# Sums of squares by 32x32 turning on VectorE, state-space values turned by VectorE and DRAM, a third of the weights' low parts on GpSimd

## The chip, the cores and the metric

One core of one Trainium2 chip runs the kernel. The metric is the device time of one execution in microseconds (us). Before the change it is 924.06 us, the median of three runs (923.71 to 925.14).

## The reference, cut to what matters

Two layers on x of 512 tokens by 1024 features. Each layer normalizes x and memory, makes one combined projection, feeds four groups of heads (retention, a Mamba-2 state-space part, stick-breaking attention, a read of 256 memory tokens), gates each group's 512 outputs, concatenates them, projects back and adds the normalized result to x.

```python
def hybrid_layer(x, mem, ...):
    hn = rmsnorm(x, pre_g)
    (ret_q, ret_k, ret_v, ret_g, xbc, z, dt_raw, sb_q, ...) = split(hn @ w_in)
    y_ret = retention(ret_q, ret_k, ret_v) * silu(ret_g)
    y_ssd = ssd_mixer(xbc, z, dt_raw, ...)
    ...
    y = concatenate([y_ret, y_ssd, y_sb, y_mem]) @ w_out
    return x + rmsnorm(y, post_g)
```

Three pieces bear on the change. Retention ends in a normalization of each of its 4 heads over 128 features. The state-space part ends in a root-mean-square norm over each of its 2 groups of 256 features. And it multiplies its convolved inputs by a step width per token and head:

```python
    # retention
    y = (y - mu) * rsqrt(var + EPS)             # mu, var over a head's 128 features
    # ssd_mixer
    xs, bm, cm = split(silu(conv(xbc) + conv_b))
    xdt = xs * delta                            # per token and head
    y_diag = (cc @ bm.T * decay_in) @ xdt       # within a chunk of 128 tokens
    states = bm.T @ (xdt * decay_states)        # one per chunk, then a running sum
    y = y_diag + (cc @ prev) * exp(a_cs) + xs * d_skip
    y = rmsnorm(y * silu(z))                    # per group of 256 features
```

## The kernel before, in words

Everything is float32, and a product of two float32 matrices is made of three matmuls: each operand is split into a high part (`h`) and a low part (`l`) of the type fp32r, and `mm3` adds `h*h`, `h*l` and `l*h`. Matmuls of this kind stand under L285 in the profile. A projection (`proj_b`) multiplies one sub-block of the weights, 1024 by 128, with all 512 tokens: 24 matmuls of 512 columns into one PSUM bank `pj`. Activations lie with features on partitions and tokens along the columns.

**Weights.** The weights of both layers are 156 sub-blocks, 78 per layer (`2 * NBLK`), of 1024 columns but for 12. ScalarE's DMA queue loads two sub-blocks at a time (`w_load`, tile `raw`). `w_prefetch` splits up to five sub-blocks ahead (`NSUB`): ScalarE casts the raw weight to `wh` (L293) and VectorE subtracts to get `wl` (L294), in 5 buffers each. After each projection one buffer of each is free for the next sub-block.

**The order of the work.** The code runs through the projections. `defer(n, f)` puts a step `f` off until `n` units later; `tick` counts one unit for each `proj_b` (two for `proj_a`) and runs what is due. A tile scheduler orders each engine's instructions when the kernel is built, by what they need and when they were written, so the order on an engine follows the units only roughly. Each engine then works in that order, one instruction behind the other, and the DMAs that SyncE (SP) issues go into its queue in its order too.

**The state-space part** (`ssd_group`, once for each of two groups, one behind the other). Its units are projections: two x blocks, a gate, B, C, a gate, two z blocks. `conv` makes a convolution of four taps with three VectorE products (L940) and a last one with a tanh (L943). The convolved values must have tokens on partitions for the products with chunk states: `ssd_values` transposes them on TensorE, 8 transposes per group of 128 by 128 by a matmul with the identity (L1003, 32 in all), into PSUM tiles `mx`, and VectorE multiplies those by the step widths (L1007) and by the decays (L1009). B is turned in another way, by `columns_turned`: VectorE's transpose of 32 by 32 blocks (`STREAM_TRANSPOSE`, L660), four DMAs on SyncE's queue that write its pieces to DRAM at their turned places (L663), and one DMA that reads the tile back (L668). `ssd_mix` multiplies the decay tiles with C by B (L1020), `ssd_states` makes three chunk states with a running product and sum on VectorE (the sum is L1033), and `ssd_out` makes the outputs (L1048 to L1056; it loads its own decays from DRAM in tiles `E`, L1041). `ssd_mix` of group 1 follows the tail of group 0 on VectorE.

**The norms.** `ssd_var` of a group, 5 units after the group's last z projection, squares both outputs on ScalarE and adds them on VectorE down to 64 partitions (L1063, L1064); it splits these into a high and a low part (L1067) and sums over the partitions with one matmul by a column of ones (`onesr`), which gives one row of 512 sums. `row_rstd` brings the row to 32 partitions of 16 values by a copy and a DMA (L811), adds epsilon and takes the power -0.5 on GpSimd (L812, L813), writes the row to DRAM (L815) and reads it back, broadcast to 128 partitions (L818, tile `r`). `ssd_norm`, 9 units after the z projection, scales the outputs by it on VectorE (L1075). Retention does the same for two heads at a time: `ret_head2` squares and adds to 32 partitions and splits, `ret_head3` makes the sums 3 units later, and `scaled` multiplies 7 units after that (L886).

GpSimd makes low parts at two places already, of activations: in `mem_head2` (L675, 16 subtractions of 128 by 512) and in `sb_head2` (L759, 24 of 256 to 512 columns).

Of the kernel before, what the change touches and what calls it, by code (L numbers as in the profile page):

```python
# [16 lines left out]
P = 128  # L17
# [117 lines left out]
def shape_constants():  # L135
    c = np.zeros((P, NCON), np.float32)
    i = np.arange(P)
    c[:, 0:128] = np.eye(P)
    c[:, 128:256] = i[:, None] <= i[None, :]
    c[:, 256:384] = 1.0  # L140
    c[:, 384:896] = np.arange(512)[None, :] < 383 + i[:, None]
    inv = np.float32(10000.0) ** (-np.arange(0, HD, 2, dtype=np.float32) / np.float32(HD))
    ang = (np.arange(SEQ, dtype=np.float32)[:, None] * inv[None, :].astype(np.float32)).T
    c[:, 896:1408] = np.concatenate([np.cos(ang), np.cos(ang)])
    c[:, 1408:1920] = np.concatenate([np.sin(ang), -np.sin(ang)])
    gam = 1.0 - 2.0 ** (-5.0 - np.arange(HEADS, dtype=np.float64))
# [4 lines left out]
    er = er.T.reshape(2, 2 * RP, RJ)  # L151
    c[:2 * RP, 1936:1968] = er.transpose(1, 0, 2).reshape(2 * RP, 2 * RJ)
    return c

BLK = 32
TT = "y"
ST, SL, SB1, SB2 = "s", "y", 2, 4
ROW = 128  # L160

# [13 lines left out]
class Builder:  # L175
# [4 lines left out]
    def __init__(self, tc, pools, args, taps=None):  # L180
        self.tc, self.nc = tc, tc.nc
        self.a = args
        self.taps = taps or {}
        self.fix, self.slots, self.small, self.wp, self.ps, self.dr = pools
        self.n = self.unit = 0
        self.todo, self.tanhs = [], []
        self.C = self.fixed(NCON + DEPTH * NPAR, F32, "consts")
        self.mhalf = self.fixed(RJ, F32, "mhalf")
        self.eps4 = self.fixed(RJ, F32, "eps4")
        self.b16 = self.fixed(2 * P, BF16, "b16")  # L190
        self.onesr = self.fixed(P, F32R, "onesr")
        self.nc.gpsimd.memset(self.mhalf[:], -0.5)
        self.nc.gpsimd.memset(self.eps4[:], EPS)

# [117 lines left out]
    def w_prefetch(self, upto=None, between=()):  # L312
        if self.starting and upto is None:
            return
        while self.w_split < (upto or min(self.nsubs, self.w_cur + self.NSUB)):
            k = self.w_split
            self.w_load(k // 2)
            n = block_width(k // 2) // 2
            h, l = (self.wp.tile([P, SUBW], F32R, tag=t, name=self.name(t), bufs=self.NSUB)[:, :n] for t in ("wh", "wl"))
            r = self.raw[k // 2]  # L320
            if isinstance(r, list):
                pieces = [(r[2 * (k % 2) + i][:], slice(512 * i, 512 * i + 512)) for i in range(2)]
            else:
# [12 lines left out]

    def w_load(self, b):
        while self.w_dma <= min(b, DEPTH * NBLK - 1):
# [461 lines left out]
        p.f = A  # L800
        return p

    def row_rstd(self, rows, eps, n=1):


        nc = self.nc
        e = self.buf(tag="r")[0:n]
        nc.scalar.copy(e, rows)
        c = self.tiny(RJ)[:n * RP]
        for i in range(n):  # L810
            nc.sync.dma_start(c[RP * i:RP * i + RP], e[i:i + 1].rearrange("o (p j) -> o p j", j=RJ))  # L811
        nc.gpsimd.tensor_tensor(out=c, in0=c, in1=eps, op=ALU.add)  # L812
        nc.gpsimd.tensor_tensor(out=c, in0=c, in1=self.mhalf[:n * RP], op=ALU.pow)  # L813
        d = self.dr.tile([n, SEQ], F32, tag=f"row{n}", name=self.name("row"), bufs=2)[:]
        nc.sync.dma_start(d.rearrange("o (p j) -> (o p) j", j=RJ), c)  # L815
        out = [self.buf(tag="r") for _ in range(n)]
        for i in range(n):
            nc.sync.dma_start(out[i], d[i:i + 1].to_broadcast([P, SEQ]))  # L818
# [32 lines left out]
    def ret_head2(self, h, v, sc, f, st, q, y):  # L851
# [10 lines left out]
        nc.scalar.copy(y, b)  # L862
        sq = self.buf(tag="r")
        nc.scalar.activation(sq, b, AF.Square, scale=HD ** -0.5)
        for n in (64, 32):
            nc.vector.tensor_add(sq[0:n], sq[0:n], sq[n:2 * n])
        if h % 2 == 0:
            self.z = self.new(512, F32R, "r"), []
# [8 lines left out]
    def ret_head3(self, i, z, ys):  # L877

        vb = self.mx()[0:2]
        self.mm(vb, self.onesr[:, 2:4], z[:], True, True)  # L880
        self.defer(7, self.scaled, ys, self.row_rstd(vb, self.con("reps", 2 * RJ, 2 * RP)[:, RJ * i:RJ * i + RJ], 2))

    def scaled(self, ys, rB):

# [74 lines left out]
    def ssd_group(self, l, g, ysb):  # L959
# [34 lines left out]
    def ssd_values(self, X):  # L994
# [1 line left out]
        nc, g = self.nc, X["g"]  # L996
        X["xdt"], X["xds"] = [], []
        for i in range(2):
            b = self.mx()
            for c in (2 * i, 2 * i + 1):  # L1000
                for j in range(2):
                    o = 256 * (c % 2) + P * j
                    nc.tensor.transpose(b[:, o:o + P], X["x"][j][:, P * c:P * c + P], self.con("ident", P))  # L1003
# [54 lines left out]
    def ssd_var(self, X):  # L1058
# [141 lines left out]
    def start(self):  # L1200
# [70 lines left out]
        self.first = self.proj_a(SSD_H, late)  # L1271
        self.mem_k2(k[1])
        self.w_load(6)
        nc.vector.tensor_copy(self.onesr[:], self.con("ones", P))

        nc.vector.tensor_copy(self.onesr[:, 2:3], self.con("tri", P)[:, 63:64])
        nc.vector.tensor_sub(self.onesr[:, 3:4], self.con("ones", 1), self.con("tri", P)[:, 63:64])

    def layer(self, l):
        self.exp_ln_phase()  # L1280
# [54 lines left out]
```

## Time and profile before

| what | value |
|---|---|
| median of three runs | 924.06 us |
| the profiled execution: its time | 923.25 us |
| its span, from the first to the last instruction | 921.5 us |
| granted TensorE clock, of full speed | 0.998 |
| low parts of weights on VectorE, 1024 wide (L294) | 144 of 1257 ns |
| all low parts of weights on VectorE | 156, 188.6 us |
| DMA rate, mean over the span | 139 GB/s |

A row of the profile's groups gives line, engine, operation, the tiles (out<-in, buffer numbers left out), partitions by elements and type, and a count; then the busy time in us and the mean of one in ns; then the idle time of that engine just before these instructions, and what ended most of it. A row of the timeline gives the start in us from the start of the span, the duration (of each, or of the whole run of like records), the engine, the line, the operation and a count; in square brackets the wait ahead of it and what ended it. A row of the chain has the same form, with the time that the chain spent there. PE is TensorE's matmul, PEld its weight load, DVE VectorE, ACT ScalarE, POOL GpSimd, SP SyncE; SPq is the DMA issue on SyncE's queue. The durations of matmul records overlap, so starts are compared and not durations.

### The profile page before, as it was taken

To read this page: it belongs to the slowest core of one execution; us is meant where nothing else is said; L and a number is where in the kernel's file an instruction comes from. 1 tells how busy PE (TensorE), PEld (TensorE's weight loads), DVE (VectorE), ACT (ScalarE), POOL (GpSimd) and SP (SyncE) were. 2 spreads that over 40 slices of the span, in tenths; PEclk is the share of its full clock that TensorE was granted. 3 is DMA by queue.
4 is the path that set the end of the run, shared out by engine and by line. 5 is a ranking of instruction groups with operands and counts; after the bars stand their busy time and mean duration, and the time that the engine had idled before them with its cause. 6 is when DMAs were issued, how large, how long until landed. Compare 5 with 4: busy or idle time off the path is not lost.

```text
span 921.5 us, 12952 instructions
## 1 busy us (share of the span) xinstructions
PE 913.2 (99%) x4667; PEld 773.6 (84%) x4667; DVE 673.3 (73%) x1081; ACT 443.5 (48%) x841; POOL 146.3 (16%) x208
## 2 busy tenths in 40 slices
PE   9999999999999999999999999999999999999997
PEld 7998888888888888888899888888888888888885
DVE  6855689888787887844587476898778869687343
ACT  6643485744453342733465336675445434335341
POOL 1200152320131110100040002423112120102001
PEclk9999999999999999999999999999999999999999
DMA  8544664642444333444345256556333362422502
GB/s 316 213 141 144 169 167 104 199 146 61 120 134 148 116 109 126 137 149 158 116 173 196 93 172 183 124 122 183 103 109 116 110 194 92 139 95 88 210 12 91
DMA packets 105408, 128.53 MB, mean 139 GB/s; under 512 B 64640, under 2 KB 79744, under 8 KB 96256
## 3 DMA queue, kind: packets, MB, share of 16 engines
q10 hardware_dynamic: 10224, 73.44, 23.4%
q1 hardware_dynamic: 95120, 54.28, 20.7%
q8 instruction: 36, 0.59, 0.3%
q14 instruction: 28, 0.23, 0.1%
HBM read 112.10 MB, written 15.56 MB: 139 GB/s over the span
## 4 chain that ended last, share of the span: by engine, by line
PE 98%; DMA 1%; ACT 0%; DVEq 0%; SPq 0%; POOLq 0%; issue 0%; POOL 0%; ACTq 0%; DVE 0%
PE pj L285 74%; PE mx L285 23%; PE mx L479 1%; DMA mem<-memT 1%; PE mx L1003 0%; ACT s L523 0%; DVEq L1331 0%; ACT s L1168 0%; POOLq L1331 0%; ACT wh L293 0%; SPq L506 0%; SPq L349 0%; SPq L1206 0%; POOL t L449 0%; ACTq L1331 0%
## 5 line engine op out<-in xcount | busy, mean ns | idle before, releaser
L285 PE MATMUL pj<-hTh,wh 128*128 128x512 f32 x704 | 276.4, 393 | 0.0
L285 PE MATMUL pj<-hTh,wl 128*128 128x512 f32 x704 | 275.8, 392 | 0.0
L285 PE MATMUL pj<-hTl,wh 128*128 128x512 f32 x704 | 274.6, 390 | 0.0
L294 DVE TENSOR_TENSOR wl<-raw,wh 128x1024 fp32r<-128x1024 f32 (+2 forms) x156 | 188.6, 1214 | 116.9 <-ACT wh L293 115.7
L293 ACT CAST wh<-raw 128x1024 fp32r<-128x1024 f32 (+2 forms) x156 | 158.7, 1020 | 205.0 <-PE pj L285 177.5
L285 PEld LDWEIGHTS pj<-hTh,wl 128*128 128x128 f32 x704 | 132.2, 188 | 27.3
L285 PEld LDWEIGHTS pj<-hTh,wh 128*128 128x128 f32 x704 | 132.3, 188 | 27.1 <-DVE s L593 0.8
L285 PEld LDWEIGHTS pj<-hTl,wh 128*128 128x128 f32 x704 | 132.3, 188 | 26.6
L285 PE MATMUL pj<-wh,s 128*128 128x512 f32 x320 | 97.6, 391 | 0.0
L285 PE MATMUL mx<-s,s 128*128 128x256 f32 (+4 forms) x528 | 79.7, 307 | 0.0
L285 PE MATMUL mx<-wh,s 128*128 128x512 f32 x256 | 79.2, 389 | 0.0
L285 PEld LDWEIGHTS mx<-s,s 128*128 128x128 f32 (+1 forms) x528 | 65.8, 177 | 8.2 <-PE pj L285 1.4
L285 PEld LDWEIGHTS pj<-wh,s 128*128 128x128 f32 x320 | 59.7, 188 | 12.4
L285 PE MATMUL pj<-wl,s 128*128 128x512 f32 x160 | 60.2, 389 | 0.0
L285 PEld LDWEIGHTS mx<-wh,s 128*128 128x128 f32 x256 | 48.1, 188 | 10.0
L294 DVE TENSOR_TENSOR s<-y,s 128x512 fp32r<-128x512 f32 x64 | 41.2, 687 | 19.7 <-ACT s L293 14.0
L262 ACT ACTIVATE s<-s 128x128 f32<-128x128 f32 (+3 forms) x96 | 41.8, 478 | 22.3 <-DVE s L733 20.6
L675 POOL TENSOR_TENSOR s<-y,s 128x512 fp32r<-128x512 f32 x16 | 23.7, 1494 | 179.9 <-ACT s L674 179.4
L293 ACT CAST s<-y 128x512 fp32r<-128x512 f32 x64 | 36.6, 617 | 30.8 <-PE mx L285 22.0
L285 PE MATMUL mx<-wl,s 128*128 128x512 f32 x128 | 49.6, 389 | 0.0
L285 PE MATMUL pj<-wl,hTh 128*128 128x256 f32 (+2 forms) x144 | 47.6, 331 | 0.0
L285 PE MATMUL pj<-wh,hTl 128*128 128x256 f32 (+2 forms) x144 | 47.5, 330 | 0.0
(185 smaller groups left out, 1298.5 us busy)
## 6 DMA issues: line engine op xcount, KB each, us to landing
raw<-wts ACTq DMA_DIRECT2D x69, 1024.0 KB, 4.8
s<-x SPq DMA_DIRECT2D x24, 256.0 KB, 4.1
y<-turned SPq DMA_DIRECT2D x24, 256.0 KB, 2.8
turned<-y SPq DMA_DIRECT2D x64, 64.0 KB, 2.2
s<-acs SPq DMA_DIRECT2D x16, 256.0 KB, 6.3
r<-row SPq DMA_DIRECT2D x12, 256.0 KB, 5.0
raw<-wts SPq DMA_DIRECT2D x4, 512.0 KB, 7.5
raw<-wts SPq DMA_DIRECT2D x2, 1024.0 KB, 6.3
```

The lines of the kernel that those rows point to most:

```text
L262: i = self.nc.scalar.activation(out, in_, func, **k)
L285: return self.nc.tensor.matmul(out, lhsT, rhs, start=start, stop=stop)
L293: self.nc.scalar.copy(h, src)
L294: self.nc.vector.tensor_sub(l, src, hf)
L479: x = self.nc.tensor.transpose(b[:, P * j:P * j + P], hn[i][:, P * j:P * j + P], self.con("ident", P))
L675: nc.gpsimd.tensor_sub(p.l, x, p.hf)
```

## The change

Four things change.

1. *State-space values.* `ssd_group` now calls `columns_turned` for the two convolved x tiles: two VectorE transposes, eight DMA writes and two DMA reads for each group, into two new tiles. `ssd_values` works on these in place in SBUF, three units after (`VD`) where it was two. The 32 transposes on TensorE are gone.
2. *Sums of squares.* The tree of additions goes down to 32 partitions. `row_rstd` takes these 32 rows (64 for a pair of retention heads), turns them in blocks of 32 by 32 on VectorE and adds along the columns with one reduction; so partition p holds the sums of the tokens p, p + 32, p + 64 and so on, 16 of them. Addition, power, write and broadcast follow as before, but the write puts each value at its own place in the row, 4 bytes apart by 128 bytes: 512 pieces, one DMA for each head. The copy, the DMA L811, the splits and the eight sums by matmul (4 of one row, 4 of two rows) are gone, with `ret_head3` and `onesr`. The table of retention's epsilons (`er`) is laid out anew to match.
3. *Units.* Retention scales 6 units (`RD`) after the second head's squares, where it was 3 + 7. `ssd_var` moves from 5 to 6 units and `ssd_norm` from 9 to 10.
4. *Low parts of weights.* `low_by_pool` names every third sub-block from the 14th on, but not those from the 16th to the 33rd of each layer's 78: 36 of the 156. For these GpSimd subtracts instead of VectorE.

TensorE has 4436 matmuls in its program where it had 4476 (40 fewer), and SyncE issues 473 DMAs where it issued 441.

```diff
+VD = 3
+RD, RT = 6, "r"
-TT = "y"
+TT, TX = "y", "s"
...
-                self.split(x, h[:, c], l[:, c], h[:, c].bitcast(F32))
+                nc = self.nc
+                nc.scalar.copy(h[:, c], x)
+                (nc.gpsimd if self.low_by_pool(k) else nc.vector).tensor_sub(l[:, c], x, h[:, c].bitcast(F32))
...
+    def low_by_pool(self, k):
+        return k > 12 and k % 3 == 2 and not 16 <= k % (2 * NBLK) < 34
...
-    def row_rstd(self, rows, eps, n=1):
+    def row_rstd(self, z, eps, n=1):
-        e = self.buf(tag="r")[0:n]
-        nc.scalar.copy(e, rows)
-        c = self.tiny(RJ)[:n * RP]
-        for i in range(n):
-            nc.sync.dma_start(c[RP * i:RP * i + RP], e[i:i + 1].rearrange("o (p j) -> o p j", j=RJ))
+        T, c = self.buf(tag=RT)[:n * RP], self.tiny(RJ)[:n * RP]
+        nc.vector.transpose(T, z)
+        nc.vector.tensor_reduce(out=c, in_=v3(T, RJ), op=ALU.add, axis=AX.X)
...
-        nc.sync.dma_start(d.rearrange("o (p j) -> (o p) j", j=RJ), c)
+        for i in range(n):
+            nc.sync.dma_start(d[i:i + 1].rearrange("o (j p) -> (o p) j", p=RP), c[RP * i:RP * i + RP])
...
     # ret_head2
-        for n in (64, 32):
-            nc.vector.tensor_add(sq[0:n], sq[0:n], sq[n:2 * n])
-        r = 64 * (h % 2)
-        nc.scalar.copy(z[r:r + 32], sq[0:32])
-        nc.vector.tensor_sub(z[r + 32:r + 64], sq[0:32], z[r:r + 32].bitcast(F32))
+        nc.vector.tensor_add(sq[0:64], sq[0:64], sq[64:128])
+        nc.vector.tensor_add(z[RP * (h % 2):RP * (h % 2) + RP], sq[0:32], sq[32:64])
-            self.defer(3, self.ret_head3, h // 2, z, ys)
+            i = h // 2
+            self.defer(RD, self.scaled, ys, self.row_rstd(z, self.con("reps", 2 * RJ, 2 * RP)[:, RJ * i:RJ * i + RJ], 2))
...
     # ssd_group
-        self.defer(2, self.ssd_values, X)
+        X["xt"] = [self.buf(tag=TX), self.buf(tag=TX)]
+        self.columns_turned(X["x"], X["xt"])
+        self.defer(VD, self.ssd_values, X)
...
-        self.defer(5, self.ssd_var, X)
-        self.defer(9, self.ssd_norm, X)
+        self.defer(6, self.ssd_var, X)
+        self.defer(10, self.ssd_norm, X)
...
     # ssd_values
-            b = self.mx()
-            ... 4 transposes into b ...
-            xdt, xds = self.buf(), self.buf()
+            b = xdt = X["xt"][i]
+            xds = self.buf()
...
     # ssd_var
-        z = self.new(512, F32R, "r")
-        nc.scalar.copy(z[0:64], sq[1][0:64])
-        nc.vector.tensor_sub(z[64:128], sq[1][0:64], z[0:64].bitcast(F32))
-        row = self.mx()[0:1]
-        self.mm(row, self.onesr[:, 0:1], z[:], True, True)
-        X["rB"], = self.row_rstd(row, self.eps4[:RP])
+        nc.vector.tensor_add(sq[0][0:32], sq[1][0:32], sq[1][32:64])
+        X["rB"], = self.row_rstd(sq[0][0:32], self.eps4[:RP])
```

The change also moves instructions, which the diff alone does not tell. Three places follow, all in layer 0 where group 1's projections run beside group 0's tail. A name's number is its tile's, given anew in each kernel, and lines of the changed kernel have their own numbers.

VectorE before, at the B convolution of group 1 (`pj_3411`, L940). L1007 and L1009 are `ssd_values` of group 1, L1055 and L1056 the end of group 0's outputs `y`, L1082 a gate, L294 a low part, L1063 the first sum of squares of `ssd_var`:

```order
L1055 TENSOR_TENSOR y_3119<-y_3119,s_3335 128x384
L1082 SCALAR_TENSOR_TENSOR y_1668<-y_1668,s_3386 128x512
L1009 TENSOR_TENSOR s_3396<-s_3395,t_713 128x256
L1007 TENSOR_TENSOR s_3406<-mx_3401,t_695 128x256 x2
L1009 TENSOR_TENSOR s_3396<-s_3395,t_713 128x256
L1056 SCALAR_TENSOR_TENSOR y_3119<-y_3119,s_3194 128x512
L1009 TENSOR_TENSOR s_3407<-s_3406,t_713 128x256
L294 TENSOR_TENSOR wl_3437<-raw_3268,wh_3436 128x1024
L940 SCALAR_TENSOR_TENSOR s_3440<-pj_3411,hp_725,s_3440 128x511
L1063 TENSOR_TENSOR r_3459<-r_3459,r_3460 128x512
```

VectorE after, at the same convolution (now `pj_3398`, L938). L1003 is now the product by the step widths, L1050 to L1052 are the outputs (L1054 to L1056 before), L941 is the convolution's end:

```order
L938 SCALAR_TENSOR_TENSOR s_3427<-pj_3398,hp_721,s_3427 128x511
L1003 TENSOR_TENSOR s_3306<-s_3306,t_691 128x256 x2
L1074 SCALAR_TENSOR_TENSOR y_1664<-y_1664,s_3394 128x512
L1003 TENSOR_TENSOR s_3307<-s_3307,t_691 128x256 x2
L938 SCALAR_TENSOR_TENSOR s_3427<-pj_3398,hp_721,s_3427 128x510
L1050 TENSOR_TENSOR s_3323<-s_3323,mx_3336 128x384
L1050 TENSOR_TENSOR s_3343<-s_3343,mx_3356 128x384
L938 SCALAR_TENSOR_TENSOR s_3427<-pj_3398,hp_721,s_3427 128x509
L1051 TENSOR_TENSOR y_3109<-y_3109,s_3323 128x384
L1051 TENSOR_TENSOR y_3110<-y_3110,s_3343 128x384
L1052 SCALAR_TENSOR_TENSOR y_3109<-y_3109,s_3142 128x512
L941 SCALAR_TENSOR_TENSOR s_3428<-s_3428,s_3427 128x512
```

Before, the outputs of group 0 were finished ahead of the first product of the convolution; now they stand behind it, with the products by the step widths. The order goes on, from the row that follows L941 and a second L1052 (L667 is B's turning, L1059 to L1061 are the sums of squares, L1005 the products by the decays, L815 and L816 the new turning and reduction):

```order
L667 STREAM_TRANSPOSE y_3437<-s_3428 128x384
L330 TENSOR_TENSOR wl_3535<-raw_3392,wh_3534 128x1024
L1059 TENSOR_TENSOR r_3492<-r_3492,r_3493 128x512
L1060 TENSOR_TENSOR r_3493<-r_3492 64x512
L1005 TENSOR_TENSOR s_3444<-s_3306,t_709 128x256 x2
L1005 TENSOR_TENSOR s_3449<-s_3307,t_709 128x256
L1061 TENSOR_TENSOR r_3492<-r_3493 32x512
L938 SCALAR_TENSOR_TENSOR s_3484<-pj_3453,hp_721,s_3484 128x511
L815 STREAM_TRANSPOSE r_3499<-r_3492 32x512
L938 SCALAR_TENSOR_TENSOR s_3484<-pj_3453,hp_721,s_3484 128x510
L330 TENSOR_TENSOR wl_3570<-raw_3392,wh_3569 128x1024
L816 TENSOR_REDUCE t_3500<-r_3499 32x16
```

Up to the reduction stand 27 instructions behind the first L938 row above (a row with x2 is two). On GpSimd, two low parts stand in a row ahead of the addition and the power that follow this reduction (`t_3500`), and two more behind them.

SyncE's queue before, from group 1's decay tiles (L986) to the broadcast of group 0's norm. L1041 loads the decays of group 0's outputs, L663 and L668 turn B of group 1:

```order
L986 DMA s_3218<-acs_722 128x512
L1041 DMA s_3315<-acs_722 64x512 x2
L1041 DMA s_3335<-acs_722 64x512 x2
L663 DMA turned_3449<-y_3450 32x12x32 x4
L668 DMA s_3448<-turned_3449 128x3x128
L811 DMA t_3472<-r_3470 32x1x16
L815 DMA row_3476<-t_3472 32x16
L818 DMA r_3478<-row_3476 128x512
```

The same stretch after (L670 and L675 are the writes and reads of `columns_turned`, L1037 the decay loads, L821 and L824 the row's write and broadcast):

```order
L986 DMA s_3207<-acs_718 128x512
L670 DMA turned_3308<-y_3309 32x16x32 x4
L670 DMA turned_3308<-y_3315 32x16x32 x4
L675 DMA s_3306<-turned_3308 128x2x256
L675 DMA s_3307<-turned_3308 128x2x256
L1037 DMA s_3323<-acs_718 64x512 x2
L1037 DMA s_3343<-acs_718 64x512 x2
L670 DMA turned_3436<-y_3437 32x12x32 x4
L675 DMA s_3435<-turned_3436 128x3x128
L821 DMA row_3505<-t_3500 32x16x1
L824 DMA r_3507<-row_3505 128x512
```

The eight writes and two reads of the x values of group 1 now stand ahead of the decay loads of group 0's outputs; the DMA from the row to 32 partitions is gone.

More of the change, by code (lines that the diff above doesn't have):

```diff
@@ L150, in shape_constants @@
     er = EPS * gam[None, :] ** (-2.0 * m[:, None])
-    er = er.T.reshape(2, 2 * RP, RJ)
+    er = er.T.reshape(2, 2, RJ, RP).transpose(0, 1, 3, 2).reshape(2, 2 * RP, RJ)
     c[:2 * RP, 1936:1968] = er.transpose(1, 0, 2).reshape(2 * RP, 2 * RJ)
     return c
+VD = 3
+RD, RT = 6, "r"
 BLK = 32
-TT = "y"
+TT, TX = "y", "s"
 ST, SL, SB1, SB2 = "s", "y", 2, 4
@@ L190, in __init__ @@
         self.b16 = self.fixed(2 * P, BF16, "b16")
-        self.onesr = self.fixed(P, F32R, "onesr")
         self.nc.gpsimd.memset(self.mhalf[:], -0.5)
@@ L864, in ret_head2 @@
         nc.scalar.activation(sq, b, AF.Square, scale=HD ** -0.5)
-        for n in (64, 32):
-            nc.vector.tensor_add(sq[0:n], sq[0:n], sq[n:2 * n])
         if h % 2 == 0:
-            self.z = self.new(512, F32R, "r"), []
+            self.z = self.buf(tag="r")[:2 * RP], []
         z, ys = self.z
-        r = 64 * (h % 2)
-        nc.scalar.copy(z[r:r + 32], sq[0:32])
-        nc.vector.tensor_sub(z[r + 32:r + 64], sq[0:32], z[r:r + 32].bitcast(F32))
+        nc.vector.tensor_add(sq[0:64], sq[0:64], sq[64:128])
+        nc.vector.tensor_add(z[RP * (h % 2):RP * (h % 2) + RP], sq[0:32], sq[32:64])
         ys.append(y)
         if h % 2:
-            self.defer(3, self.ret_head3, h // 2, z, ys)
[L877 to L881, printed above, removed]
+            i = h // 2
+            self.defer(RD, self.scaled, ys, self.row_rstd(z, self.con("reps", 2 * RJ, 2 * RP)[:, RJ * i:RJ * i + RJ], 2))
     def scaled(self, ys, rB):
@@ L998, in ssd_values @@
         for i in range(2):
-            b = self.mx()
[L1000 to L1003, printed above, removed]
-            xdt, xds = self.buf(), self.buf()
+            b = xdt = X["xt"][i]
+            xds = self.buf()
             for c in (2 * i, 2 * i + 1):
@@ L1273, in start @@
         self.w_load(6)
-        nc.vector.tensor_copy(self.onesr[:], self.con("ones", P))
-        nc.vector.tensor_copy(self.onesr[:, 2:3], self.con("tri", P)[:, 63:64])
-        nc.vector.tensor_sub(self.onesr[:, 3:4], self.con("ones", 1), self.con("tri", P)[:, 63:64])
     def layer(self, l):
```

## The prediction

> **What bounds the kernel now.** The page comes first: its span, the engine line and the chain of work that ended last.
>
> ```profile
> span 921.5 us, 12952 instructions
> PE 913.2 (99%) x4667; PEld 773.6 (84%) x4667; DVE 673.3 (73%) x1081; ACT 443.5 (48%) x841; POOL 146.3 (16%) x208
> PE 98%; DMA 1%; ACT 0%; DVEq 0%; SPq 0%; POOLq 0%; issue 0%; POOL 0%; ACTq 0%; DVE 0%
> ```
>
> TensorE holds 98% of that chain. A busy TensorE can hide short waits, so the view of waits on TensorE is next; this is its longest group, and the warm-up's.
>
> ```profile
> PE mx L285 <- POOL b L197: 1.2, 1, 1.2
> ```
>
> So the time is the sum of the matmul starts. An instruction taken from TensorE shortens the run by its start-to-start time; work added to another engine costs nothing until TensorE waits for it.
>
> **What leaves TensorE.** The timeline of TensorE gives the price of a transpose and of a 1-row or 2-row sum, and the groups by shape give their counts.
>
> ```profile
> 322.07 0.39 PE L285 MATMUL pj<-hTh,wl 128*128 128x512 f32 x1
> 322.31 0.82 PE L1003 MATMUL mx<-consts,s 128*128 128x128 f32 x6
> 322.88 0.48 PE L285 MATMUL pj<-hTh,wh 128*128 128x512 f32 x1
> 323.19 0.40 PE L285 MATMUL pj<-hTl,wh 128*128 128x512 f32 x1
> 338.43 0.40 PE L285 MATMUL mx<-r,onesr 128*1 128x512 f32 x1
> 338.66 0.39 PE L285 MATMUL pj<-hTh,wl 128*128 128x512 f32 x1
> L1003 PE MATMUL mx<-consts,s 128*128 128x128 f32 x32 | 5.1, 272 | 0.0
> L285 PE MATMUL mx<-r,onesr 128*1 128x512 f32 x4 | 1.6, 398 | 0.0
> L285 PE MATMUL mx<-r,onesr 128*2 128x512 f32 x4 | 1.6, 396 | 0.0
> ```
>
> From 322.07 to 323.19 stand two 512-column matmuls and six transposes: 1.12 us. Twenty-four such matmuls take 5.44 us in the chain (its row is below), 0.23 each, so six transposes cost 1.12 - 0.45 = 0.67, one 0.11; 32 of them 3.5 us. The eight sums with ones cost 0.23 each (338.43 to 338.66), 1.9 us. TensorE loses **5.4 us**. That is an upper bound of the gain: nothing else in the change shortens TensorE.
>
> **A third of the low parts on GpSimd.** The rows are the weight's low and high part, the chain while a projection runs, and GpSimd subtracting two widths.
>
> ```profile
> L294 DVE TENSOR_TENSOR wl<-raw,wh 128x1024 fp32r<-128x1024 f32 x144 | 180.5, 1257 | 111.5 <-ACT wh L293 110.4
> L293 ACT CAST wh<-raw 128x1024 fp32r<-128x1024 f32 x144 | 151.4, 1053 | 198.2 <-PE pj L285 173.4 <-PE mx L285 15.3 <-DVE s L951 3.9
> 140.02 5.44 PE pj L285 x24
> 150.62 1.30 POOL L759 TENSOR_TENSOR s<-y,s 128x512 fp32r<-128x512 f32 x1 [7.17 <-ACT s L758]
> 154.10 0.74 POOL L759 TENSOR_TENSOR s<-y,s 128x256 fp32r<-128x256 f32 x1
> ```
>
> GpSimd takes 0.28 us per 128 columns (1.30 - 0.74 for 256), so a 1024-wide part takes 1.30 + 4 x 0.28 = 2.42 us against VectorE's 1.26, and 36 parts move (the rule of the new function over 156 parts). ScalarE waits 173 us for the projection that frees a buffer: a part is made as soon as a buffer is free, four projections of 5.44 us ahead, and 1.05 + 2.42 us fit into 21.8. I cost the parts themselves at nothing; without that cover it would be 36 x 1.16 = 42 us. Behind them in GpSimd's order stand the two additions and powers of each norm; ScalarE's next weight load, which is queued ahead of its later casts, waits for a part up to 1.16 us longer than today, inside the 173 us.
>
> VectorE and GpSimd do disturb each other:
>
> ```profile
> 124.30 4.13 POOL L675 TENSOR_TENSOR s<-y,s 128x512 fp32r<-128x512 f32 x2 [0.82 <-ACT s L674]
> 125.47 1.81 DVE L294 TENSOR_TENSOR wl<-raw,wh 128x1024 fp32r<-128x1024 f32 x1
> ```
>
> Two GpSimd parts took 4.13 instead of 2 x 1.30, and VectorE's part beside them 1.81 instead of 1.26. On VectorE's stretch below, this matters: between nothing and one whole part, 2.4 us. I take **1.8**, because one part (the one made just ahead of the addition in GpSimd's order) lies in the stretch and most of VectorE's instructions there read two SBUF tiles, as this one does. The Trainium skill (SBUF — State Buffer, "Who interferes with whom") has the same as a rule: a VectorE instruction with two SBUF inputs and a GpSimd one that reads SBUF exclude each other for the whole instruction. By that rule the stretch would pay up to the full 2.4; the two rows agree in kind.
>
> **The norm of group 0, the place where TensorE may wait.** In both layers, VectorE's scaling of group 0 (L1075) stands ahead of the decay products (L1020) and the running states (L1033) of group 1, and TensorE needs those. The rows, in layer 0:
>
> ```profile
> 329.23 0.75 DVE L940 SCALAR_TENSOR_TENSOR s<-pj,hp,s 128x511 f32<-128x511 f32 x1
> 343.27 2.90 POOL L813 TENSOR_TENSOR t<-t,mhalf 32x16 f32<-32x16 f32 x1
> 346.20 0.32 SPq L815 DMA_DIRECT2D row<-t  x1
> 349.59 0.33 SPq L818 DMA_DIRECT2D r<-row  x1
> 353.14 1.42 DVE L1075 SCALAR_TENSOR_TENSOR y<-y,consts,r 128x512 f32<-128x512 f32 x2 [2.52 <-DMA r<-row]
> 359.78 0.41 DVE L1033 TENSOR_TENSOR s<-s,mx 128x256 f32<-128x256 f32 x1
> 360.93 3.85 PE L285 MATMUL mx<-s,s 128*64 128x128 f32 x44
> ```
>
> Today the last state is ready at 360.19. TensorE's 44 records from 360.93 end at 364.53, and the first that need this state come after about 18 of them, an estimate of 362.4: a margin of 2.2 us.
>
> After the change the squares stand later. The new order on VectorE puts the outputs of group 0 (L1050 to L1052) behind the first product of the B convolution, today's row at 329.23, where they now stand ahead of it. Up to the end of the new reduction I count 27 instructions behind that product, priced by these groups:
>
> ```profile
> L940 DVE SCALAR_TENSOR_TENSOR s<-pj,hp,s 128x510 f32<-128x510 f32 x16 | 12.0, 748 | 0.4
> L1054 DVE TENSOR_TENSOR s<-s,mx 128x384 f32<-128x384 f32 x8 | 4.4, 548 | 0.0
> L1009 DVE TENSOR_TENSOR s<-s,t 128x256 f32<-128x256 f32 x12 | 5.0, 418 | 0.1
> L745 DVE STREAM_TRANSPOSE s<-s 128x512 f32<-128x512 f32 x8 | 5.5, 689 | 3.3 <-POOL s L736 3.3
> L780 DVE TENSOR_REDUCE t<-pj 128x4 f32<-128x512 f32 x8 | 5.4, 678 | 2.1 <-PE pj L285 2.1
> ```
>
> The time goes by the columns. Nine instructions of 512 (the turning and the reduction among them) are 6.2 us, four convolution products 3.0, five of 384 2.75, seven of 256 2.9, two weight parts 2.5: 17.4. Neighbours overlap by 0.08 (two products take 1.42, not 1.50), so 15.2, and 0.4 for four steps that wait for the one just before them. 329.23 + 0.67 + 15.6 = 345.5. Addition and power 3.2: 348.7; today 346.17, although the change cuts out the high and low part of the sum, TensorE's sum, a copy and one DMA.
>
> Row write and broadcast took 346.20 to 353.14 here. The new write scatters 512 values of 4 bytes. For it I take 2.6 us, between the two groups nearest to it (512 runs of 128 bytes, 64 KB; 32 runs of 64 bytes, 2 KB):
>
> ```profile
> turned<-y SPq DMA_DIRECT2D x64, 64.0 KB, 2.2
> row<-t SPq DMA_DIRECT2D x4, 2.0 KB, 3.6
> ```
>
> It is nearest to the first in the number of pieces; ends 2.2 and 3.6. With 3.5 for the broadcast, VectorE scales at 354.9 and has the last state 7.05 later, as today: 361.9. TensorE needs it at 362.4 less one removed sum, 362.2 (other removed work lies before 329.23 and moves both alike). Margin 0.3; with 1.8 for GpSimd a **wait of 1.5 us in each layer**, between none and 2.1 (3.1 with the slow write too).
>
> **The other edits.** Retention's sums lose TensorE's step as well, and their scaling moves from ten units after the squares to six. Today:
>
> ```profile
> 272.95 0.80 SPq L818 DMA_DIRECT2D r<-row  x2
> 296.14 1.28 DVE L886 TENSOR_TENSOR y<-y,r 128x512 f32<-128x512 f32 x2
> ```
>
> The broadcasts are issued 23 us before use: free, and if that cover went, a few us per pair on VectorE's queue. VectorE gives up 36 x 1.26 = 45 us and takes 24 turnings and eight reductions of 0.7, 22 us: free, at 73% busy. SyncE issues 32 DMAs more; where they stand is the third rival.
>
> **The sum.** 923.25 us is the profiled execution, 921.5 of it span. 923.25 - 5.4 + 2 x 1.5 = 920.85. The median of before, 924.06, lies 0.8 above that execution, so I predict **921.6** as a median.
>
> **Rivals.** A difference within 0.2% (1.85 us) can't be told from none. The bounds in medians are 922.2 and 925.9.
>
> *No wait at all*: GpSimd disturbs elsewhere and the margin holds. For it: 0.3 us of margin is left without the disturbance. 924.06 - 5.4 = 918.7. Chance 0.22.
>
> *The gain is eaten*: the rule of exclusion in full, 2.4 us in the stretch, and a row write as slow as today's, 3.4. Wait 2.4 + 0.8 - 0.3 = 2.9 per layer, 924.06 - 5.4 + 5.8 = 924.5. For it: the two rows of disturbance; against: only part of 2.4 falls on a working VectorE. Chance 0.25.
>
> *Slower, by SyncE's order*: the decay loads of group 0's outputs (L1041) are issued long before use today. Now they stand behind eight writes and two reads of the turned values of group 1, and the first read waits until the writes have landed.
>
> ```profile
> 319.62 0.69 DVE L943 SCALAR_TENSOR_TENSOR s<-s,s 128x512 f32<-128x512 f32 x1 [0.76 <-ACT s L267]
> ...
> L1041 SPq DMA_DIRECT2D s<-acs x16: 445/540/597, 299.7 to 804.2; - x16
> ...
> DMA to landing us min/median/max: 3.0/4.6/5.3
> ```
>
> The last answer is for these loads. The same line for writes of the kind (L663):
>
> ```profile
> DMA to landing us min/median/max: 1.5/2.9/5.7
> ```
>
> I take 0.54 us for each issue. The second value is ready at 320.3, turned at 321.0; last write issued 322.6, landed 325.5; two reads issued by 326.6, the last load at 328.2, landed 332.8. VectorE comes to its product (L1054) six instructions behind the one at 329.23, four of 256 columns, one of 512 and a convolution product: 329.23 + 0.67 + 1.7 + 0.7 + 0.7 = 333.0. So the margin is 0.2 at the medians. With writes and loads at their longest, the loads come 2.8 + 0.7 - 0.2 = 3.3 too late; with the 1.5 above, a wait of 4.8 per layer: 924.06 - 5.4 + 9.6 = 928.3. It decides from 3.6 us per layer on, where it passes 925.9. For it: the margin is thin, and the writes of 64 KB come four at a time; against: it takes more than medians. Chance 0.22.
>
> **The numbers.** The forecast itself has 0.31, so faster is 0.31 + 0.22 = 0.53, same 0.25, slower 0.22. The range goes from 918.5, just under no wait, to 927.0, inside the third rival between its bound of 925.9 and its price of 928.3; I put 0.14 above it and 0.04 below, for a gain that I don't see.
>
> **What would show it.** Right: no L1003 transposes and no onesr rows on TensorE; 1024-wide parts on GpSimd of 2.4 us; a wait of TensorE for VectorE of 1 to 2 us at the states of group 1, once in each layer; VectorE's scaling of group 0 waiting for the row. Wrong: TensorE waiting for a weight's low part; a row write over 4 us; VectorE waiting for decay loads ahead of L1050; or no wait in the middle of a layer, which gives the first rival.

## The result, and the profile after

The changed kernel takes 967.98 us (median of five runs, 967.39 to 972.35) against 923.73 us before (five runs): 1.0497 times as long, with a 95% interval of 1.0484 to 1.0510. That is 44 us slower; 921.6 was forecast, in a range of 918.5 to 927.0, with a chance of 0.22 for slower.

The page of the changed kernel shows where the bound went:

```profile
span 965.8 us, 12902 instructions
PE 928.7 (96%) x4627; PEld 783.2 (81%) x4627; DVE 664.8 (69%) x1058; ACT 430.4 (45%) x821; POOL 243.1 (25%) x244
PEclk9999999999999898999999999999999998999999
PE 76%; DVE 9%; DMA 8%; POOL 2%; issue 2%; ACT 2%; SPq 1%; DVEq 0%; ACTq 0%; POOLq 0%
```

TensorE carried 98% of the chain, and now 76%. Two numbers of this page against those of before split the loss. TensorE's idle time is span less busy time: 965.8 - 928.7 = 37.1 us, where it was 8.3, so 28.8 more. And it is busy for 15.5 us longer although 40 matmuls worth 5.4 us are gone: the rest is slower by 20.9. 28.8 + 20.9 - 5.4 = 44.3, the whole difference of the spans. The granted clock, all nines before, has eights; its mean is 0.979 where it was 0.998. Spread over the spans that is 965.8 x 0.021 = 20.3 us of lost clock against 921.5 x 0.002 = 1.8, so the clock accounts for some 18.5 of the 20.9 us. Where the rest comes from is open.

The view of waits on TensorE has new groups:

```profile
PE mx L286 <- DVE s L1029: 8.5, 2, 4.3
PE mx L286 <- DMA s<-turned: 5.6, 3, 2.2
PE mx L286 <- issue: 4.8, 2, 2.6
PE mx L286 <- ACT s L294: 4.0, 2, 2.0
PE pj L286 <- DVE s L938: 3.0, 1, 3.0
PE pj L286 <- DVE s L295: 2.8, 2, 2.0
```

TensorE waits for VectorE more than for anything else: 14.3 of these 28.7 us. The views of waits on VectorE and on SyncE's queue say what those wait for in their turn:

```profile
DVE y L1067 <- DMA r<-row: 45.7, 4, 13.6
DVE s L988 <- DMA s<-acs: 36.3, 4, 12.0
...
SPq L824 <- DMA row<-t: 45.3, 9, 6.7
```

Before, VectorE waited 13.9 us for broadcast rows and 5.2 us for decay loads, and SyncE 18.6 us for row writes. In the changed kernel SyncE stands still for 45.3 us, in nine waits, until a row has landed in DRAM (L821, 512 pieces of 4 bytes), since it can issue the broadcast (L824) only then; all that it issues later waits as well. The line of the row writes, of after and then of before, has the time from issue to landing:

```profile
DMA to landing us min/median/max: 5.8/6.4/7.1
```

```profile
DMA to landing us min/median/max: 1.7/2.2/5.4
```

One stretch shows the whole mechanism: the chain in the retention stretch of layer 0 of the changed kernel (start, duration, what; rows left out are under 1 us).

```profile
246.19 0.61 DVE t L816
...
247.16 3.35 POOL t L818
...
250.52 5.80 DMA row<-t
...
256.96 0.38 SPq L675
...
257.94 8.15 DMA s<-acs
...
266.11 0.73 DVE s L988 x2
```

The sums of a pair of retention heads are ready at 246.8, the power at 250.5; the row lands 5.8 us after its issue. Only then come the read of a turned tile (256.96, L675) and the decay loads of the state-space part (257.94, L986), which before stood ahead of any row on SyncE's queue, as its timeline has it:

```profile
250.50 0.38 SPq L668 DMA_DIRECT2D s<-turned  x1
250.98 1.84 SPq L986 DMA_DIRECT2D s<-acs  x4
```

VectorE has the subtraction on the first decay tile (L988) at the head of its queue and stands for 11.82 us:

```profile
266.11 1.38 DVE L988 TENSOR_TENSOR s<-s,t 128x512 f32<-128x512 f32 x2 [11.82 <-DMA s<-acs]
```

A convolution stands behind it, and the chain runs on through that to the matmul at 282.60, ahead of which TensorE waited 1.97 us. The late turned read makes TensorE wait directly: 2.12 us, until 262.43. Both rows are in the list of waits below.

**The clock.** What a wait costs is not its length alone. Here is the longest wait of layer 0, in windows of the changed kernel (the last columns are PEclk, DMA share, GB/s):

```profile
323.04 4.77 PE L286 MATMUL mx<-s,s 128*128 128x128 f32 x26 [4.13 <-DVE s L1029]
...
300.00:318.00 18.00, 16.65 (x86) 13.68 (x86) 9.64 (x14) 4.73 (x7) 3.16 (x3) 1.00 0.65 158
318.00:323.00 5.00, 0.91 (x12) 0.55 (x8) 4.99 (x7) 1.89 (x3) 2.06 (x2) 1.00 0.00 0
323.00:331.00 8.00, 7.90 (x35) 6.26 (x36) 6.54 (x10) 3.46 (x5) 2.35 (x1) 0.57 0.48 147
331.00:340.00 9.00, 9.00 (x42) 7.42 (x41) 3.92 (x5) 1.31 (x3) 0.00 (x0) 1.00 0.55 148
```

After a wait of 4.13 us TensorE runs for 8 us at a mean clock of 0.57 and loses about 3.4 us more (8 x 0.43). These are five of the other waits of layer 0 on TensorE's timeline; one of 0.80 us and two under 1.3 us in the first ten microseconds are left out:

```profile
262.43 1.23 PE L286 MATMUL mx<-r,s 128*128 128x128 f32 x4 [2.12 <-DMA s<-turned]
282.60 0.90 PE L286 MATMUL mx<-s,s 128*128 128x256 f32 x3 [1.97 <-ACT s L294]
307.96 1.53 PE L286 MATMUL mx<-s,s 128*128 128x256 f32 x6 [1.35 <-DMA s<-turned]
378.04 2.38 PE L286 MATMUL mx<-s,s 128*64 128x128 f32 x18 [2.62 <-issue]
420.05 0.73 PE L286 MATMUL pj<-wh,s 128*128 128x512 f32 x2 [1.98 <-DVE s L295]
```

In windows of 1 us, the clock fell to 0.50 after those of 2.12, 1.97 and 2.62 us and stayed at 1.00 after those of 1.35 and 1.98 us. Summed over these windows, 1.7 us of clock were lost after 2.12 and 1.97 us, and 3.4 us after 2.62 and 4.13 us; at half clock that is a stretch of 3.4 us, or twice that. The Trainium skill (TensorE: Matmul & The Clock Gate, "What's actually happening") tells of such a gate: half rate after an idle window of about 3.4 us that runs free of the program, full rate after a busy one. The halving and its length, one or two such windows, agree with the trace. That waits of 2 us, shorter than the window, were enough at times doesn't.

### The profile page after: what moved, and what is told of

Its sections match the earlier page's. It is cut to its first block, busy times and chain, and to the rows that moved or that the text cites. A ratio compares the mean times of both kernels' runs of the same rounds, so it can differ in the third digit from the quotient of the medians.

```text
span 965.8 us, 12902 instructions
## 1 busy us (share of the span) xinstructions
PE 928.7 (96%) x4627; PEld 783.2 (81%) x4627; DVE 664.8 (69%) x1058; ACT 430.4 (45%) x821; POOL 243.1 (25%) x244
## 4 chain that ended last, share of the span: by engine, by line
PE 76%; DVE 9%; DMA 8%; POOL 2%; issue 2%; ACT 2%; SPq 1%; DVEq 0%; ACTq 0%; POOLq 0%
PE pj L286 56%; PE mx L286 19%; DMA row<-t 3%; DMA s<-acs 3%; POOL t L818 2%; DVE wl L330 1%; DVE s L1016 1%; DVE s L938 1%; DVE s L988 1%; PE mx L486 1%; DVE y L884 1%; DVE s L295 1%; DMA raw<-wts 1%; DMA mem<-memT 1%; DVE s L805 0%
## 5 line engine op out<-in xcount | busy, mean ns | idle before, releaser
L286 PE MATMUL pj<-hTl,wh 128*128 128x512 f32 x704 | 277.8, 395 | 0.0
L330 DVE TENSOR_TENSOR wl<-raw,wh 128x1024 fp32r<-128x1024 f32 (+2 forms) x120 | 146.9, 1229 | 81.1 <-ACT wh L329 67.5
L286 PEld LDWEIGHTS pj<-hTh,wh 128*128 128x128 f32 x704 | 134.3, 191 | 31.1 <-issue 3.4
L330 POOL TENSOR_TENSOR wl<-raw,wh 128x1024 fp32r<-128x1024 f32 (+1 forms) x36 | 88.9, 2470 | 280.5 <-ACT wh L329 280.4
L286 PE MATMUL mx<-s,s 128*128 128x256 f32 (+4 forms) x528 | 91.4, 342 | 18.9 <-DVE s L1029 8.5
L286 PEld LDWEIGHTS mx<-s,s 128*128 128x128 f32 (+1 forms) x528 | 73.6, 198 | 30.9 <-DVE s L1029 10.0
L295 DVE TENSOR_TENSOR s<-y,s 128x512 fp32r<-128x512 f32 x64 | 48.3, 799 | 18.7 <-ACT s L294 15.0
L294 ACT CAST s<-y 128x512 fp32r<-128x512 f32 x64 | 36.0, 617 | 38.7 <-PE mx L286 20.4
```

Source lines behind the costliest of these rows:

```text
L286: return self.nc.tensor.matmul(out, lhsT, rhs, start=start, stop=stop)
L294: self.nc.scalar.copy(h, src)
L295: self.nc.vector.tensor_sub(l, src, hf)
L330: (nc.gpsimd if self.low_by_pool(k) else nc.vector).tensor_sub(l[:, c], x, h[:, c].bitcast(F32))
```

## The experiments

The theory at the start: the norms' row write is slow and stands, with the broadcasts, ahead of the decay loads and turned reads on SyncE's queue, and this makes the loss. The rivals: the low parts on GpSimd, and the turned values on SyncE's queue. Ratios are to the kernel before on the same chip, with 95% intervals.

**Each part alone.** The edits, to the kernel before in the first three:

```diff
# e1: only this
+                (nc.gpsimd if self.low_by_pool(k) else nc.vector).tensor_sub(l[:, c], x, h[:, c].bitcast(F32))
# e2: only columns_turned(X["x"], X["xt"]), ssd_values in place at 3 units
# e3: only the new row_rstd, its callers and units
# e4: the changed kernel with
+        return False        # low_by_pool
```

> The kernel before with one change alone: 36 low parts of weights on GpSimd. Theory (the norms' row write of 6.4 us, and its place on SyncE's queue ahead of the decay loads and the turned reads, makes the loss): this part is almost harmless, 922 to 927 us, GpSimd parts of about 2.5 us, TensorE's waits under 4 us in total. Rival (GpSimd and VectorE exclude each other in SBUF, GpSimd's powers become longer, the low parts are the loss): 940 us or more, TensorE waiting for low parts or for VectorE.

> The kernel before with one change alone: the state-space values turned by VectorE and DRAM, three units ahead. Theory (row write): 920 to 925 us, since 32 transposes of 3.5 us leave TensorE and the old norms keep their place. Rival (the eight writes and two reads per group on SyncE's queue delay the decay loads): 935 us or more, with VectorE waiting for decay loads by 5 us or more per group.

> The kernel before with the new sums of squares alone (turning, reduction, scattered row write, the new units); transposes stay on TensorE, low parts on VectorE. Theory (row write): it holds most of the loss, 950 to 968 us, row writes landing after 5.8 us or more, VectorE waiting over 20 us in total for the decay loads behind them. Rivals (low parts, or turned values): 919 to 927 us.

> The changed kernel with all low parts back on VectorE. Theory (row write): 955 to 968 us. Rival (low parts on GpSimd): 918 to 930 us, and GpSimd's powers back at 3 us.

| kernel | us | before | ratio |
|---|---|---|---|
| low parts alone | 925.47 | 923.43 | 1.0026 (1.0016 to 1.0036) |
| turned values alone | 944.91 | 923.43 | 1.0224 (1.0204 to 1.0245) |
| sums alone | 959.07 | 923.43 | 1.0387 (1.0366 to 1.0408) |
| all but the low parts | 962.37 | 923.43 | 1.0422 (1.0406 to 1.0437) |

The low parts alone are not it: 2 us, GpSimd's parts at 2455 ns (2.42 us was worked out) and VectorE's at 1266 instead of 1257; TensorE's waits were 5.4 us in total, over the 4 expected. The sums are most of it, within what the theory gave. Leaving the low parts out of the changed kernel takes 0.0075 off the ratio, 7 us, so beside the other parts they cost more than alone. But the turned values lose 21.5 us by themselves, with the old norms: the theory missed that. The parts alone add to 59 us, more than the 44 together.

The rival for this run had the time but not the wait: VectorE waits for decay loads only 1.7 us in all. What it waits for instead is in the view of waits on VectorE of that kernel, and the timeline shows the longest:

```profile
DVE s L1005 <- DMA s<-turned: 18.9, 7, 4.4
...
336.26 1.57 DVE L1005 TENSOR_TENSOR s<-s,t 128x256 f32<-128x256 f32 x4 [4.36 <-DMA s<-turned]
```

VectorE stands at the products by the step widths (L1005) before the turned values have come back from DRAM. It is the scheduler that puts them there: with five units instead of three in the code (built, not run) these products come at the same places in VectorE's order.

**The sums: the write or the place?** Two edits of the kernel with the sums alone. In the first the row is written in another order, in larger pieces, so that the factors come out at other tokens; it is there for its time alone. In the second the row comes later, as before the change.

```diff
# f2
-            nc.sync.dma_start(d[i:i + 1].rearrange("o (j p) -> (o p) j", p=RP), c[RP * i:RP * i + RP])
+            nc.sync.dma_start(d[i:i + 1].rearrange("o (p j) -> (o p) j", j=RJ), c[RP * i:RP * i + RP])
# f3: in ret_head2, and ret_head3 with row_rstd and defer(7, self.scaled, ...)
-            self.defer(RD, self.scaled, ys, self.row_rstd(...))
+            self.defer(3, self.ret_head3, i, z, ys)
```

> The sums alone (as in the run with only the new sums), but the row goes to DRAM as 32 pieces of 64 bytes instead of 512 of 4 bytes; the factors then come out at other tokens, the work is the same. Theory (the 4-byte pieces make the row write slow, and all that SyncE issues behind it waits): writes land after 2 to 3.5 us instead of 8.1, time 919 to 932 us. Rival (not the write's length but the norms' new place on SyncE's queue, ahead of the decay loads): 945 us or more.

> The sums alone, with the scattered write, but retention's turning and row come 3 units after the second head's squares and the scaling 7 later, as before the change. Theory (slow write, wherever it stands): only the two waits in retention's stretch may shrink, 940 to 957 us, and the wait at group 0's scaling (11.1 us on VectorE) stays. Rival (new place on the queue): 919 to 930 us.

With the contiguous row: 921.86 against 923.02 us, 0.9986 (0.9977 to 0.9995). Its writes landed so, against those of the sums alone (second fence):

```profile
DMA to landing us min/median/max: 1.3/3.4/4.5
```

```profile
DMA to landing us min/median/max: 6.9/8.1/10.9
```

One line of code turns a loss of 35.6 us into a gain of 1.2. The new place on the queue is kept: SyncE issues its DMAs in the same order in both traces, through the state-space part of layer 0. The theory's number is met; the rival of the place alone is out. But the place counts while the write is slow: with the row later, 935.04 us, 1.0124 (1.0107 to 1.0141), so 24 of the 35.6 us go, more than the theory had. What is left is the wait that it named, at group 0's scaling, with a convolution's end behind it for which TensorE waits 4.97 us:

```profile
352.90 1.42 DVE L1073 SCALAR_TENSOR_TENSOR y<-y,consts,r 128x512 f32<-128x512 f32 x2 [11.56 <-DMA r<-row]
```

**The values: VectorE's order or SyncE's?** Two edits of the kernel with the turned values alone:

```diff
# f4
-        self.defer(3, self.ssd_values, X)
+        self.defer(4, self.ssd_values, X)
-                nc.vector.tensor_tensor(out=v3(xdt[:, s], 4), ...)
+                self.tc.keep_in_program_order(nc.vector.tensor_tensor(out=v3(xdt[:, s], 4), ...))
# f5: f4, and the loads of E moved from ssd_out to the start of ssd_group
+        X["E"] = [self.buf(), self.buf()]
+        ... the four dma_start of S["rows"][1, ...] into X["E"][i] ...
```

> The turned values alone, with the products by the step widths pinned on VectorE behind the C convolution (4 units) instead of where the scheduler puts them. Theory A (VectorE comes to the products before the turned values have landed, and everything behind waits): 918 to 925 us. Theory B (the eight writes and two reads hold back the decay loads of group 0's outputs): VectorE waits 5 us or more per layer for decay loads ahead of the outputs instead, 930 to 948 us.

> As the run with pinned products, and the decay loads of a group's outputs are issued at the group's start, ahead of the turned values. Theory A and theory B both give 918 to 925 us; the difference to the run without early loads is what theory B is worth. Over 930 us would speak against both.

Pinned: 931.60 against 923.02 us, 1.0100 (1.0085 to 1.0115). With the loads first too: 920.26 us, 0.9971 (0.9960 to 0.9982). So, in this order, the pinned place (theory A) is worth about 13 us and the early loads (theory B) 11. A alone does not reach the gain; B alone was not run. Theory B works in another way than it was expected to: the wait for decay loads is only 1.61 us in layer 0, not 5 or more. The timelines show what else it does, of the pinned kernel first and then of the one with early loads:

```profile
332.56 0.56 DVE L1053 TENSOR_TENSOR s<-s,mx 128x384 f32<-128x384 f32 x1 [1.61 <-DMA s<-acs]
...
349.43 0.77 PE L285 MATMUL pj<-hTh,wh 128*128 128x512 f32 x1 [2.97 <-DVE s L940]
```

```profile
318.86 0.55 DVE L1055 TENSOR_TENSOR s<-s,mx 128x384 f32<-128x384 f32 x1
```

With late loads the first product of group 0's outputs runs at 332.56, and the rest of the outputs falls among group 1's convolutions; TensorE waits 2.97 us for one of these, in each layer. With early loads the same product runs at 318.86, and the view of waits on TensorE has no group of such a kind left.

**Two by two.** Last, the two causes together, each as the change has it or mended, all with the low parts on GpSimd; and the version with both mended and the low parts on VectorE. The mended row is turned back by VectorE one unit after the power, and written in 16 pieces of 128 bytes:

```diff
+        self.defer(1, self.row_back, w, n, out)
+    def row_back(self, w, n, out):
+        r = self.tiny(32)[:n * RP]
+        self.tc.keep_in_program_order(nc.vector.transpose(r, w))
...
+            nc.sync.dma_start(d[i:i + 1].rearrange("o (j p) -> (o j) p", p=RP), r[RP * i:RP * i + RJ])
```

> The whole change, but the row goes to DRAM as 32 pieces of 64 bytes (the factors then come out at other tokens, the work is the same). If the parts add up: 923.0 + 2.4 (low parts) + 21.5 (values) - 1.2 (sums with this write) = 945.7 us, 941 to 951. If the scattered write were behind the values' loss too when all stand together: 920 to 932 us.

> The whole change with the scattered row write, but the values mended (products pinned, decay loads first); low parts on GpSimd. It is the fourth cell beside the changed kernel (968.0), the one with a contiguous row (928.5) and the one with both mended (920.6). If the scattered write decides by itself: 950 to 962 us. If write and values only do harm together: 919 to 932 us.

> The same with the 36 low parts on GpSimd. If the low parts cost what they cost alone (2.4 us): 919.5 to 922.5 us. If they only cost where GpSimd's power of a norm stands behind them and a norm is awaited: the same as without them, 917 to 920 us.

> Sums and turned values both, mended: the factors are turned back by VectorE one unit later, so that the row is written as 16 pieces of 128 bytes; the products by the step widths are pinned behind the C convolution; the decay loads are issued at the group's start; low parts stay on VectorE. Theory (the loss came from the scattered row write, VectorE's place for the products and SyncE's order, and from nothing else): the 5.4 us taken from TensorE come out, 917 to 920 us. Rival (the added work on VectorE and SyncE costs time wherever it stands): 922 us or more.

| low parts on GpSimd | values as changed | values mended |
|---|---|---|
| scattered row | 967.98, 1.0497 | 957.60, 1.0380 (1.0358 to 1.0402) |
| row in larger pieces | 928.51, 1.0055 (1.0040 to 1.0071) | 920.56, 0.9974 (0.9965 to 0.9983) |

The two cells of the lower row do not have the same row write: on the left it is 32 pieces of 64 bytes, with the factors at other tokens, on the right the mended one. By the ratios the scattered row decides by itself: 41 us in the first column and 37 in the second. The values are worth 7 to 11 us in either row, not the 21.5 that they cost alone; the sum of parts was wrong there (945.7 worked out, 928.51 measured). The waits show the difference: alone, VectorE waited 18.9 us for turned values, in seven waits; in the kernel of 928.51 it waits 4.1, in two. Why is open. That the old norms had a matmul of TensorE behind VectorE's late work, which the new sums lack, would fit: with the values alone TensorE waited 4.8 us at it. It was not tried.

With both mended and the low parts on VectorE: 918.79 against 922.91 us, 0.9955 (0.9942 to 0.9967), 4.1 us faster and the best of all. Its row writes land after 1.6 us, and its waits on TensorE are those of before:

```profile
DMA to landing us min/median/max: 1.3/1.6/3.8
```

```profile
PE mx L286 <- POOL b L198: 1.2, 1, 1.2
PE pj L286 <- ACT s L530: 1.0, 2, 0.7
```

The low parts on GpSimd take 1.8 of it back (920.56, same chip), nearly the 2.0 that they cost alone.

**Why the row write is slow.** The kernel before with 40 added writes of four forms came first:

> The kernel before with 40 more DMA writes to DRAM, one per projection in the attention stretch, ten of each form: (a) 512 pieces of 4 bytes, neighbours in DRAM from neighbouring partitions, as in the new row write; (b) 512 pieces of 4 bytes, each 128 bytes from the next; (c) 512 pieces of 128 bytes; (d) 32 pieces of 64 bytes. Theory 1 (neighbouring pieces in one line get in each other's way): a lands after 6 to 8 us, b, c and d after 1.5 to 3.5. Theory 2 (a 4-byte piece is slow as such): a and b both 6 to 8 us. Theory 3 (only load from other transfers made it slow): a below 4 us.

It settled nothing: the writes were issued in bunches, one behind the other, and all four medians came out at 6.9 to 8.5 us; only the shortest landings differed (6.9 us for form a, 1.9 to 2.2 for the others). So two kernels followed with ten writes each, of one form:

```diff
+    def pieces(self, u):
+        d = self.dr.tile([512, 32], F32, ...)[:]
# h2: neighbours
+        out = d.rearrange("a b -> (a b)")[0:512].rearrange("(j p) -> p j", p=32)
# h3: 128 bytes apart
+        out = d.rearrange("(j p) b -> p j b", p=32)[:, :, 0]
+        self.tc.keep_in_program_order(self.nc.sync.dma_start(out, self.C[0:32, 896:912]))
```

> The kernel before with ten more writes, one every fourth projection, all of 512 pieces of 4 bytes that are neighbours in DRAM. If they are slow without other such writes about: 5.5 us or more at the least and at the median. If it was the bunch: about 2 us.

> The same ten writes, with the pieces of 4 bytes 128 bytes apart. If neighbours get in each other's way: a median of 2 to 3 us. If a 4-byte piece is slow as such: 5.5 us or more, as with neighbours.

The landings, neighbours first:

```profile
DMA to landing us min/median/max: 7.0/8.4/13.6
```

```profile
DMA to landing us min/median/max: 2.2/3.2/7.1
```

Same count, same size, same source, one execution of each kernel; only the distance in DRAM differs. So it is not the 4 bytes as such. Nor is it that neighbours come from different partitions: the row of before has that with 32 pieces of 64 bytes for each head (its writes land after 2.2 us) and the mended row with 16 of 128 bytes (1.6 us). What is slow here is pieces of 4 bytes that are neighbours in DRAM. The Trainium skill (DMA: Bandwidth & Descriptors, "Specifications") says that below 512 bytes the engines read, modify and write; by that size alone both forms would be equally slow, and they are not. That such reads and writes of neighbours come one behind the other would explain the difference, but no run shows it.

## Why the prediction was wrong

**The step that failed first** was the row write: "For it I take 2.6 us, between the two groups nearest to it", with ends of 2.2 and 3.6. It took 6.4 us (5.8 to 7.1), outside both ends. A row write over 4 us was also its own sign of being wrong. The two groups were nearest by the number of pieces and by their bytes, but neither had pieces of 4 bytes that are neighbours in DRAM, and those are slow (8.4 against 3.2 us with distance between them). A number between two rows is no bound when the new form differs from both in the same way.

**The step that made it 40 us** was "The other edits": "The broadcasts are issued 23 us before use: free". This looked at who uses the broadcasts and not at what SyncE issues behind them. The new sums no longer wait for three units and a matmul, so the row and its broadcasts moved ahead of a turned read and the decay loads in the order (L821 and L824 ahead of L986), and VectorE comes to these before they have landed. The third rival had the mechanism and the sign, SyncE's order holding back decay loads, but at the loads of group 0's outputs. In the changed kernel VectorE has no wait for those; issuing them early was worth 11 us in the pinned runs. And its price of 928.3 had neither the slow row nor the half clock in it.

**The values' own way** was not priced at all: when the turned values are back, and where VectorE has their products in its order. The third rival used the landing of the writes for the decay loads behind them, and the same sum gives the values: reads issued by 326.6 and some 3 us to land, 329.6, with the products (L1003 in the changed kernel) just behind a product at 329.23. There was no margin there.

**A wait's price** was taken as its length. The longest wait on TensorE in the trace of before is 1.2 us, so the half clock after one of 2 us could not be read from it; it is some 18.5 of the 44.3 us.

**What was right**: the 40 matmuls were priced at 5.4 us, as an upper bound; with both causes mended TensorE is busy for 5.1 us less (908.1 against 913.2) and 4.1 us came out. GpSimd's parts took 2.5 us, and the low parts were hidden as parts. The 1.8 us per layer for GpSimd's disturbance was not borne out where the low parts stand alone: they cost 2.0 us in all, where TensorE waited 2.8 us in two waits, and not at the states of group 1 but at those of group 0. What it was in the changed kernel no run separates from the rest of their 7 us. The wait forecast at group 1 is there, ahead of the 44 matmuls from 378.04 (the row above has the first 18, up to the end of that view's window), 2.62 us in layer 0 instead of 1.5, as one of several.

## What to carry to other kernels

When a change moves a chain of dependent DMAs on an in-order queue, list everything that is now issued behind its waits, with the first instruction that needs each; a chain that is itself early enough can still hold back one that is not. Before scattering small values into DRAM, turn them on chip so that each partition writes a contiguous run: one short transposition took the row write from 6.4 to 1.6 us. And where a scheduler orders the engines, pin the users of a DRAM round trip behind work that covers it, and count TensorE waits of about 2 us and more at more than their length: here 28.8 us of idle time came with 20.9 us of slower matmuls.

## What the runs showed of the hardware that was not expected

- 512 pieces of 4 bytes land after 8.4 us when they are neighbours in DRAM, and after 3.2 us when they are 128 bytes apart (medians of ten writes).
- Single waits of TensorE of 1.97 to 4.13 us were followed by 3.4 or 6.8 us at a granted clock of 0.50; one of 1.98 us was not.
- GpSimd's subtractions of 128 by 1024 left the mean of VectorE's low parts nearly as it was (1266 against 1257 ns), although the trace of before has a place where two such instructions slowed each other.
